# A feed-forward's down products computed by a second pass through DRAM, with seven instead of eight products

## The chip, the core and the metric

The kernel runs on one core of a Trainium2 chip. Its engines work side by side, each through its own queue of instructions in order: TensorE (PE) for matmuls, VectorE (DVE), ScalarE (ACT) and GpSimd (POOL) for everything element by element, SyncE (SP) mostly for issuing DMAs. The metric is the device time of one execution in microseconds (us), median of several.

## What is computed

One layer of an encoder, on 2048 tokens of one request and 256 of another (2304 in all, 1024 channels), in float32. Two mixers (a bidirectional mLSTM and an attention) come first and are not changed. The change lies in the last part of the layer and the final norm:

```python
x = x + jnp.concatenate([m_out, a_out], axis=-1) @ w_out
h = rmsnorm(x, norm2_w)
u = centred_dwconv(h @ w_up, conv_w, conv_b)      # 1024 -> 2 x 2816, width-3 convolution over tokens
a, g = jnp.split(u, 2, axis=-1)
x = x + (jax.nn.silu(g) * a) @ w_down             # 2816 -> 1024
return rmsnorm(x, final_norm_w)
```

The convolution is zero padded at the ends of each request.

## The kernel before

Channels lie on the 128 partitions and tokens along the free dimension. Every matmul is done three times: each operand is split into a rounded high part (a copy by ACT) and the rest (a difference, mostly by DVE), and high x high, high x low and low x high are summed in PSUM. The instructions are ordered at build by a scheduler that works with its own estimates of their durations; at run time every engine keeps that order.

Stage c (`phase_c`, L995) multiplies the mixed heads with `w_out`, nine blocks of 256 tokens, adds x, writes x to DRAM (`x1_d`, L1050) and the normed n2 to DRAM (`n2_d`, L1065). The operand tiles alternate between two rings (L1023).

The feed-forward (`phase_d`, L1221) runs over three blocks of 768 tokens (`BLK`). In each block the channels of the gate and of a go in 11 groups of two tiles (256 of 2816). The up product of two tiles and 1024 inputs is done as 2 x 2 blocks in seven products instead of eight (`up_start`, L1162): token halves and input halves give sums and differences. The sums of n2 are made once for a block by `n2_sums` (L1136): SP loads, POOL sums, SP stores to `n2t_d`, four calls, spread over groups 3 to 6 of the block before (L1348), or over stage c for the first block. `n2_load` (L1114) loads and splits the seven operands ("11", "21", "t2", "t1", "t3", "22", "t4"); three are loaded early, four at the start of the feed-forward, all seven anew at a block change. The sums of the weights are made by POOL for each pair of tiles (L1189 to L1192). Each of the seven weight tiles is split by ACT (L1180) and DVE (L1181) and used by 4 x 3 matmuls of 386, 384 or 382 columns (L1184). The products add up in three of four PSUM banks, and are copied out and added by ACT (L1200) and DVE (L1203) as the sums allow; "t2", "t3" and "t4" continue in the bank of "11".

The convolution (`conv`, L1265) is one ACT instruction (L1271) and two DVE instructions (L1278) a tile, with the tokens at a block's edge kept in `carry`. Then y (L1358) is silu(g) x a, split into `act` (L1363, L1364); `w_down` is loaded by SP (L1367) and split (L1373, L1374).

The down products (`down`, L1316) of a group are done one group later: 8 output tiles x 2 token parts, each 2 x 3 matmuls of 384 columns (L1322) in four banks of their own, added by DVE to accumulators in SBUF that hold x (L1324). So PE alternates between up and down products. After the last group of a block, `finish` (L1286) squares, sums, takes the power -0.5, spreads it over the partitions by matmuls (L142) and scales (L1312); SP stores y. In the last block the last two groups' down products go in three parts of 256 columns.

## Time and profile before

| | us |
|---|---|
| time, median of 3 runs | 3429.92 (3428.42 to 3431.00) |
| span of the profiled execution, first to last instruction | 3427.2 |
| feed-forward, from its first up matmul (1830.4) to the end | 1596.8 |
| one of the four groups from 2113.9 to 2299.7 | 46.5 |

The profiled execution's own time is known as its span; the median lies 2.7 us above it. A row such as "PE 3329.3 (97%) x20058" gives busy time, share of the span and number of instructions. PEld is the loading of weights into PE, which overlaps with matmuls. Matmuls overlap too, so their listed durations (some 338 ns for 384 columns) are longer than their distance in time; the distance is what counts, and is read from a number of them in a row. A "<-" behind an idle time names the instruction that ended it.

### The profile page before, as it was taken

To read this page: it belongs to the slowest core of one execution; us is meant where nothing else is said; L and a number is where in the kernel's file an instruction comes from. 1 tells how busy PE (TensorE), PEld (TensorE's weight loads), DVE (VectorE), ACT (ScalarE), POOL (GpSimd) and SP (SyncE) were. 2 spreads that over 40 slices of the span, in tenths; PEclk is the share of its full clock that TensorE was granted. 3 is DMA by queue.
4 is the path that set the end of the run, shared out by engine and by line. 5 is a ranking of instruction groups with operands and counts; after the bars stand their busy time and mean duration, and the time that the engine had idled before them with its cause. 6 is when DMAs were issued, how large, how long until landed. Compare 5 with 4: busy or idle time off the path is not lost. (4 is left out here: it accounts for less than half of the span.)

```text
span 3427.2 us, 55596 instructions
## 1 busy us (share of the span) xinstructions
PE 3329.3 (97%) x20058; PEld 3098.4 (90%) x20058; DVE 2677.3 (78%) x4654; ACT 1931.2 (56%) x4329; POOL 1120.9 (33%) x1328
## 2 busy tenths in 40 slices
PE   7989999999999999899999999999999999999998
PEld 6878888888888888688899999999999999999998
DVE  6885687777768788967767878789888888888776
ACT  4536666666666767655544444446444446555554
POOL 6653132213232323211244333226233224322222
PEclk9999999999999999999999999999999999999999
DMA  6765342333345444422365232223323213421221
GB/s 220 243 203 159 89 140 86 115 123 98 108 131 160 143 123 139 145 77 94 101 216 198 81 105 87 68 80 133 129 94 103 72 59 128 140 74 62 69 74 50
DMA packets 254756, 404.27 MB, mean 118 GB/s; under 512 B 32112, under 2 KB 156816, under 8 KB 254480
## 3 DMA queue, kind: packets, MB, share of 16 engines
q1 hardware_dynamic: 226576, 358.23, 32.7%
q0 software_dynamic: 11344, 33.04, 3.6%
q10 hardware_dynamic: 16560, 9.44, 0.9%
q8 instruction: 158, 2.59, 0.3%
q14 instruction: 118, 0.97, 0.1%
HBM read 316.73 MB, written 83.90 MB: 117 GB/s over the span
## 5 line engine op out<-in xcount | busy, mean ns | idle before, releaser
L1322 PE MATMUL pd<-act,wd 128*128 128x384 f32 (+1 forms) x3120 | 593.4, 336 | 23.9 <-DVE acc L1324 12.6
L1322 PEld LDWEIGHTS pd<-act,wd 128*128 128x128 f32 x3120 | 539.6, 188 | 32.6 <-DVE acc L1324 18.1
L601 DVE TENSOR_TENSOR pl<-ps,ph 128x512 fp32r<-128x512 f32 x520 | 352.7, 683 | 181.5 <-ACT ps L600 173.4
L1184 PE MATMUL pa<-nt,wut 128*128 128x386 f32 (+2 forms) x2376 | 454.3, 339 | 0.0
L599 ACT ACTIVATE ph<-ps 128x512 fp32r<-128x512 f32 x520 | 309.4, 595 | 243.5 <-PE ps L596 239.5
L1184 PEld LDWEIGHTS pa<-nt,wut 128*128 128x128 f32 x2376 | 421.6, 190 | 0.3 <-ACT u L1200 0.3
L570 DVE TENSOR_REDUCE mx<-px 128x1 f32<-128x512 f32 (+1 forms) x528 | 345.5, 670 | 74.4 <-PE px L569 72.4
L1278 DVE SCALAR_TENSOR_TENSOR y<-u,cw,y 128x768 f32<-128x768 f32 (+1 forms) x264 | 315.6, 1196 | 36.4 <-ACT y L1271 29.3
L1189 POOL TENSOR_TENSOR tw<-ru 128x512 f32<-128x512 f32 x66 | 94.1, 1425 | 732.5 <-DMA ru<-w_up 558.5
L613 PE MATMUL pv<-ph,v 128*128 128x512 f32 (+1 forms) x1040 | 319.4, 401 | 1.0 <-ACT ph L599 0.8
L600 ACT ACTIVATE ps<-ps 128x512 f32<-128x512 f32 x520 | 310.3, 597 | 0.0
L1200 ACT ACTIVATE u<-pa 128x386 f32<-128x386 f32 (+2 forms) x264 | 128.3, 486 | 320.9 <-PE pa L1184 320.7
L1324 DVE TENSOR_TENSOR acc<-pd,acc 128x384 f32<-128x384 f32 (+1 forms) x544 | 280.3, 535 | 35.5 <-PE pd L1322 34.1
L1041 PEld LDWEIGHTS po<-cmx,wo 128*128 128x128 f32 x1728 | 220.7, 191 | 8.2 <-DVE mmx L931 0.6
L1041 PE MATMUL po<-cmx,wo 128*128 128x256 f32 x1728 | 224.2, 284 | 0.4 <-DVE mmx L931 0.4
L595 PE MATMUL ps<-qq,kk 128*128 128x512 f32 x520 | 215.5, 416 | 4.2 <-DVE mx L570 2.4
L569 PE MATMUL px<-kk,qq 128*128 128x512 f32 (+1 forms) x528 | 202.8, 413 | 6.0 <-DVE mx L570 2.9
L596 PE MATMUL ps<-qm,kl 65*128 65x512 f32 x520 | 206.7, 399 | 0.0
L759 PE MATMUL mj<-mn,wm 128*128 128x256 f32 x1296 | 203.0, 289 | 2.8 <-ACT og L773 1.9
L759 PEld LDWEIGHTS mj<-mn,wm 128*128 128x128 f32 x1296 | 187.1, 193 | 19.8 <-ACT og L773 2.0
L769 PEld LDWEIGHTS mv<-wm,mn 128*128 128x128 f32 x1296 | 182.8, 190 | 18.4 <-ACT qb L765 2.5
L769 PE MATMUL mv<-wm,mn 128*128 128x256 f32 x1296 | 196.5, 285 | 1.0 <-ACT qb L765 0.9
(288 smaller groups left out, 7266.6 us busy)
## 6 DMA issues: line engine op xcount, KB each, us to landing
ru<-w_up SPq DMA_DIRECT2D x132, 512.0 KB, 3.4
mn<-n_d SPq DMA_DIRECT2D x216, 256.0 KB, 3.4
rd<-w_down SPq DMA_DIRECT2D x66, 512.0 KB, 3.6
n_d<-n1T SPq DMA_DIRECT2D x18, 1024.0 KB, 5.6
dm<-nm_d POOLq DMA_DIRECT2D x72, 256.0 KB, 4.1
mjn<-n_d SPq DMA_DIRECT2D x72, 256.0 KB, 3.3
mvn<-n_d SPq DMA_DIRECT2D x72, 256.0 KB, 3.1
q_d<-qz SPq DMA_DIRECT2D x18, 512.0 KB, 3.7
```

The lines of the kernel that those rows point to most:

```text
L570: nc.vector.tensor_reduce(s.mx[:, t, z0:z0 + 1], ps[:, 0:w], AX.X, ALU.max)
L599: nc.scalar.activation(ph, ps, AF.Exp)
L600: nc.scalar.activation(ps, ps, AF.Exp)
L601: nc.vector.tensor_tensor(pl, ps, f32(ph), ALU.subtract)
L613: nc.tensor.matmul(s.pv[0:HD if k in (1, 3) else P, 0:N], v, p, start=(kp == 0 and k == 0), stop=(2 * kp + 2 == s.nk and k == 5))
L759: nc.tensor.matmul(pj[:, o], s.w[c][:, a, o * P:(o + 1) * P], nT[c][:, :, h, :], start=(c + o + k == 0), stop=(c == NCC - 1 and k == 2 and ...
L769: nc.tensor.matmul(pv[:, o], nT[c][:, o, a, :], s.w[c][:, h, 256:512], start=(c + o + k == 0), stop=(c == NCC - 1 and k == 2 and o == 1))
L1041: nc.tensor.matmul(po[:, o], wo[z // 2][c][:, a, n], mx[c][:, h, :], start=(c == 0 and k == 0), stop=(c == NCC - 1 and k == 2))
L1184: nc.tensor.matmul(p, w[:, aa, c, :], ops[k][:, c, bb, 0:n], start=c == 0 and i == 0 and not add, stop=c == NCC // 2 - 1 and i == 2, skip_ ...
L1278: nc.vector.scalar_tensor_tensor(y[:, s:e], u[:, s + k:e + k], cw[:, k, jj:jj + 1], y[:, s:e], ALU.mult, ALU.add)
L1322: nc.tensor.matmul(po, wds[j][c // 4][:, aa, c % 4 * P:(c % 4 + 1) * P], acts[j][:, bb, z0:z1], start=(j == 0 and k == 0), stop=(j == len( ...
L1324: nc.vector.tensor_tensor(accs[c][:, z0:z1], po, accs[c][:, z0:z1], ALU.add)
```

## The change

The feed-forward becomes two passes. The up pass (`phase_u`) runs over two blocks of 1152 tokens. Each of the seven products is now 2 x 12 matmuls of 290 or 286 columns into a pair of banks, in a ring of four pairs that takes all eight banks; u22 is added by DVE directly from PSUM. From silu(g) x a of a group (two tiles, two token halves of 576) POOL makes the sums for seven down products and stores seven tiles of [128, 576] to DRAM (`a_d`). Nothing of the down product is done in this pass.

The down pass (`phase_e`) then runs over the seven products, in the order of `DOPS`. For each it goes over three stretches of 384 columns (1152 columns stand for both halves of both blocks) and 11 pairs of tiles, with 4 x 3 matmuls a pair, into two pairs of banks; the four result quadrants stay in SBUF and are updated after each stretch. Weights are loaded and split once, in a ring of 13; four of the seven weight tiles are sums, made by POOL in the first stretches and taken through DRAM (`s_d`). Operands come back from `a_d` by SP, four pairs at a time, split by ACT and DVE. POOL adds x and sums the squares; the norm follows in the steps after a stretch is complete.

Besides: `n2_sums` now issues its loads and stores from POOL, in halves, in a ring of three shared with the sums of the up pass; all splits of operands at the block change and the start go to DVE; x1 and n2 have other layouts (n2 in two tensors that overlap by 256 tokens); the two rings of stage c are swapped; rings and pools are placed in memory in a chosen order. The diff, cut to its core:

```diff
-BLK = 768
+BLK = 1152
...
-LAGO = 2
-AB = 3
-NH = 386
+NH = 580
 NW = 2 * NH + 1
-DT = (0, 2 * NH, 2 * NH + BLK, T)
+DT = (0, 2 * NH, T)
+HB = BLK // 2
+TW = T // 2
+N2A, N2B = 1280, 1024
+NP = NFC // 2
+CG = 384
 APRI = 1000
 WB = 8
 RST = 512
...
-WD = 4
 YB = 3
 UB = 3
 RW = 4
-PO = 4
-PB = 4
+WRA = 6
+WRB = 7
+TR = 4
+DW = 4
+TG = 4
+WA = 2
 PHB = 6
 PLB = 6
 PLAG = 2
-ZT = 3
 SG = 3
-RS = 2
 V, G = "vector", "gpsimd"
-P0 = ((V, G),) * 4
-P1 = ((V, G),) * 7
+P0 = ((V, V),) * 4
+P1 = ((V, V),) * 7
...
-                if n % 2:
+                if n % 2 == 0:
...
-            g.st.dma_start(g.x1_d[b, :, 2 * z - 2:2 * z + 2], x[:, 2 * z - 2:2 * z + 2])
+            g.st.dma_start(g.x1_d[:, 2 * z - 2:2 * z + 2, b * BT:(b + 1) * BT], x[:, 2 * z - 2:2 * z + 2])
...
-                g.st.dma_start(g.n2_d[:, z - 3:z + 1, b * BT:(b + 1) * BT], x[:, z - 3:z + 1])
+                if b * BT < N2A:
+                    g.st.dma_start(g.n2_d[0][:, z - 3:z + 1, b * BT:(b + 1) * BT], x[:, z - 3:z + 1])
+                if b * BT >= N2B:
+                    g.st.dma_start(g.n2_d[1][:, z - 3:z + 1, b * BT - N2B:(b + 1) * BT - N2B], x[:, z - 3:z + 1])
...
-            if n > 4 and sums:
+            if (n, z) > (5, 0) and sums:
...
-def n2_sums(g, pool, b, c, engs=("gpsimd",) * 4, tag="raw", bufs=RW):
+def n2_sums(g, pool, b, c, engs=("gpsimd",) * 4, tag="tc", bufs=3):
 
 
     nc = g.nc
     n = (DT[b + 1] - DT[b]) // 2
-    rs = []
-    for k in range(2):
-        r = pool.tile([P, D if tag == "raw" else 2 * NH], F32, tag=tag, name=f"rn{b}_{c}_{k}", bufs=bufs)[:, 0:2 * n]
-        r = r.rearrange("p (h t) -> p h t", h=2)
-        nc.sync.dma_start(r, g.n2_d[:, c + NCC // 2 * k, DT[b]:DT[b + 1]].rearrange("p (h t) -> p h t", h=2))
-        rs.append(r)
-    (b11, b12), (b21, b22) = ((r[:, 0], r[:, 1]) for r in rs)
-    for eng, (o, p, q) in zip(engs, ((b11, b12, b11), (b12, b22, b12), (b22, b22, b11), (b21, b21, b22))):
-        getattr(nc, eng).tensor_tensor(o, p, q, ALU.subtract)
-    for k in range(2):
-        g.st.dma_start(g.n2t_d[b, k, :, c, :, 0:n], rs[k])
-
-
-def up_load(g, s1, b, jj):
-
-    rs = [s1.tile([P, D], F32, tag="raw", name=f"ru{b}_{jj + k}", bufs=RW) for k in range(2)]
+    m = n // 2
+    for z in range(2):
+        rs = []
+        for k in range(2):
+            r = pool.tile([P, NH], F32, tag=tag, name=f"rn{b}_{c}_{z}_{k}", bufs=bufs)[:, 0:n]
+            r = r.rearrange("p (h t) -> p h t", h=2)
+            src = g.n2_d[b][:, c + NCC // 2 * k, DT[b] - (0, N2B)[b]:DT[b + 1] - (0, N2B)[b]].rearrange("p (h t) -> p h t", h=2)
+            nc.gpsimd.dma_start(r, src[:, :, z * m:z * m + m])
+            rs.append(r)
+        (b11, b12), (b21, b22) = ((r[:, 0], r[:, 1]) for r in rs)
+        for eng, (o, p, q) in zip(engs, ((b11, b12, b11), (b12, b22, b12), (b22, b22, b11), (b21, b21, b22))):
+            getattr(nc, eng).tensor_tensor(o, p, q, ALU.subtract)
+        for k in range(2):
+            nc.gpsimd.dma_start(g.n2t_d[b, k, :, c, :, z * m:z * m + m], rs[k])
+
+
+def up_load(g, pools, b, jj):
+
+    pool = pools[g.nup % 2]
+    g.nup += 1
+    rs = [pool.tile([P, D], F32, tag="raw", name=f"ru{b}_{jj + k}", bufs=2) for k in range(2)]
...
+def banks(g, pool, name):
+
+    k = g.nbank = g.nbank + 1
+    return pool.tile([P, 2, 512], F32, tag=f"p{k % 2}", name=name, bufs=1)
...
     def mul(p, k, src, add=False):
 
-        w = s1.tile([P, 2, NCC // 2, P], F32R, tag="wu", name=f"wu{k}_{nm}", bufs=WU)
+        i = g.nwu = (g.nwu + 1) % WU
+        w = s1[i // 3].tile([P, 2, NCC // 2, P], F32R, tag="wu", name=f"wu{k}_{nm}", bufs=3 if i < 3 else WU - 3)
         hi, lo = (w[:, a].rearrange("p c n -> p (c n)") for a in range(2))
         nc.scalar.activation(hi, src, AF.Copy)
         nc.vector.tensor_tensor(lo, src, f32(hi), ALU.subtract)
-        for c in range(NCC // 2):
-            for i, (aa, bb) in enumerate(((0, 0), (0, 1), (1, 0))):
-                nc.tensor.matmul(p, w[:, aa, c, :], ops[k][:, c, bb, 0:n], start=c == 0 and i == 0 and not add,
-                                 stop=c == NCC // 2 - 1 and i == 2, skip_group_check=add)
-    p1, p2 = bank("a"), bank("b")
+        for z in range(2):
+            for c in range(NCC // 2):
+                for i, (aa, bb) in enumerate(((0, 0), (0, 1), (1, 0))):
+                    nc.tensor.matmul(p[:, z], w[:, aa, c, :], ops[k][:, c, bb, z * m:z * m + m],
+                                     start=c == 0 and i == 0 and not add, stop=c == NCC // 2 - 1 and i == 2,
+                                     skip_group_check=add)
+    p1, p2 = bank("a" + nm)[:, :, 0:m], bank("b" + nm)[:, :, 0:m]
...
-        copy(u22, p1)
-        add(u22, u22, u21)
+        add(u22, p1, u21)
...
+            def store(k, gi, t):
+                nc.gpsimd.dma_start(g.a_d[gi // TG][DOPS.index(k), :, gi % TG, b * HB:(b + 1) * HB], t)
...
+                for y, yg in zip(yas, ygs):
+                    nc.vector.tensor_tensor(y, y, yg, ALU.mult)
+                b11, b12, b21, b22 = (y[:, k * HB:(k + 1) * HB] for y in yas for k in range(2))
+                t1, t2, t4 = (sa.tile([P, NH], F32, tag="tc", name=f"tc{k}_{b}_{gi}", bufs=3)[:, 0:HB] for k in (1, 2, 4))
+                store("11", gi, b11)
+                nc.gpsimd.tensor_tensor(t1, b12, b11, ALU.subtract)
+                nc.gpsimd.tensor_tensor(t2, b22, t1, ALU.subtract)
+                for k, t in (("t2", t2), ("21", b21), ("t1", t1)):
+                    store(k, gi, t)
+                nc.gpsimd.tensor_tensor(b12, b22, b12, ALU.subtract)
+                nc.gpsimd.tensor_tensor(t4, b21, t2, ALU.subtract)
+                for k, t in (("t3", b12), ("22", b22), ("t4", t4)):
+                    store(k, gi, t)
+
+
...
+def phase_e(g, tc, pd):
...
+    G3 = TW // CG
+    with ExitStack() as st:
...
+        quad = {k: sc.tile([P, 4, TW], F32, name="c%d%d" % k) for k in ((0, 1), (0, 0), (1, 0), (1, 1))}
...
+        def halves(t, src):
+            lo, hi = t[:, 1], t[:, 0]
+            nc.scalar.activation(hi, src, AF.Copy)
+            nc.vector.tensor_tensor(lo, src, f32(hi), ALU.subtract)
+
+        def down(f, o, p):
+            return g.w_down[0, (2 * p + f) * P:(2 * p + f + 1) * P, o * h:o * h + h]
+
+        SRC = {"11": (0, 0), "21": (1, 0), "t4": (1, 1)}
+        SUM = {"t1": 0, "t2": 1, "t3": 2, "22": 3}
+
+        def sums_load(p):
+            r = sy.tile([P, 4, h], F32, tag="x", name=f"ds{p}", bufs=2)
+            for k, (f, o) in enumerate(((0, 1), (1, 1), (0, 0), (1, 0))):
+                nc.gpsimd.dma_start(r[:, k], down(f, o, p))
+            return r
+
+        def sums(p, r):
+            b12, b22, b11, b21 = (r[:, k] for k in range(4))
+            nc.gpsimd.tensor_tensor(b22, b12, b22, ALU.add)
+            nc.gpsimd.tensor_tensor(b12, b11, b12, ALU.subtract)
+            nc.gpsimd.dma_start(g.s_d[SUM["t1"]][p], b22)
+            nc.gpsimd.tensor_tensor(b11, b22, b11, ALU.subtract)
+            nc.gpsimd.dma_start(g.s_d[SUM["t3"]][p], b12)
+            nc.gpsimd.tensor_tensor(b21, b21, b11, ALU.subtract)
+            nc.gpsimd.dma_start(g.s_d[SUM["t2"]][p], b11)
+            nc.gpsimd.dma_start(g.s_d[SUM["22"]][p], b21)
+
+        nw = [0]
+
+        def weight(i, p):
+            k = DOPS[i]
+            n = nw[0] % (WRA + WRB)
+            nw[0] += 1
+            w = (swa if n < WRA else swb).tile([P, 2, h], F32R, tag="w", name=f"we{k}_{p}", bufs=WRA if n < WRA else WRB)
+            r = sr.tile([P, h], F32, tag="dw", name=f"dw{k}_{p}", bufs=DW)
+            nc.sync.dma_start(r, down(*SRC[k], p) if k in SRC else g.s_d[SUM[k]][p])
+            halves(w, r)
+            return w
+
+        TS = [(p, min(p + TG, NP)) for p in range(0, NP, TG)]
+
+        def acts(i, z, q):
+            p0, p1 = TS[q]
+            t = sx.tile([P, 2, TG, CG], F32R, tag="t", name=f"te{DOPS[i]}_{z}_{q}", bufs=TR)[:, :, 0:p1 - p0]
+            nc.sync.dma_start(f32(t[:, 1]), g.a_d[q][i, :, :, z * CG:(z + 1) * CG])
+            halves(t, f32(t[:, 1]))
+            return t
...
+        def resid(o, hf, z):
+            x = sy.tile([P, 4, h], F32, tag="x", name=f"xe{o}{hf}_{z}", bufs=2)[:, :, 0:CG]
+            for c, n, t in spans(hf, z):
+                nc.sync.dma_start(x[:, :, c:c + n], g.x1_d[:, 4 * o:4 * o + 4, t:t + n])
+            a = C(o, hf)[:, :, z * CG:(z + 1) * CG]
+            nc.gpsimd.tensor_tensor(a, a, x, ALU.add)
+
+        done = set()
+
+        def squares(o, hf, z, ms=(0, 1, 2, 3)):
+            q = sy.tile([P, 4, h], F32, tag="x", name=f"qe{o}{hf}_{z}_{ms[0]}", bufs=2)[:, 0:len(ms), 0:CG]
+            nc.scalar.activation(q, C(o, hf)[:, ms[0]:ms[-1] + 1, z * CG:(z + 1) * CG], AF.Square, scale=1.0 / 32.0)
+            return [q[:, m] for m in range(len(ms))]
...
+        def norm(hf, z, extra=()):
+            ps = banks(g, pd[(g.nbank + 1) // 2 % 2], f"r{hf}_{z}")
+            sqs = [sms[hf, z], *extra]
...
+            for c in range(NCC):
+                a = C(c // 4, hf)[:, c % 4, z * CG:(z + 1) * CG]
+                nc.vector.scalar_tensor_tensor(a, a, g.fw[:, c:c + 1], r, ALU.mult, ALU.mult)
+                for c0, n, t in spans(hf, z):
+                    g.st.dma_start(g.yT[c, :, t:t + n], a[:, c0:c0 + n])
+
+        UPD = {"11": [((0, 1), None)], "21": [((0, 0), (0, 1))], "t4": [((1, 0), None)], "t2": [((0, 1), (0, 1))],
+               "t3": [((1, 1), (0, 1))], "t1": [((0, 1), (0, 1)), ((1, 1), (1, 1))], "22": [((0, 1), (0, 1))]}
...
+        fetch_w(WA)
+        fetch_t(2)
...
+        for p in range(NP):
+            if p + 1 < NP:
+                at(4 * p, lambda p=p: load_sums(p + 1))
+            at(4 * p + 1, lambda p=p: sums(p, sr4[p]))
+        for z in range(G3):
+            e = 2 * SZ + z * NP
+            at(e + 3, lambda z=z: resid(0, 0, z))
+            at(e + 8, lambda z=z: collect(0, z, squares(0, 0, z)))
+            e = 4 * SZ + (z + 1) * NP
+            at(e + 1, lambda z=z: resid(1, 0, z))
+            at(e + 3, lambda z=z: resid(0, 1, z))
+            at(e + 6, lambda z=z: collect(0, z, squares(1, 0, z)))
+            at(e + 14, lambda z=z: norm(0, z))
...
+        for i, k in enumerate(DOPS):
+            for z in range(G3):
+                end = i == 6 and z == G3 - 1
+                ps = [banks(g, pd[(g.nbank + 1) // 2 % 2], f"e{k}_{z}_{m}")[:, :, 0:CG] for m in range(2)]
+
+                def mul(p, ms):
+                    w, t = ws[i, p], ts[i, z, p // TG][:, :, p % TG]
+                    for m in ms:
+                        for n, (aa, bb) in enumerate(((0, 0), (0, 1), (1, 0))):
+                            nc.tensor.matmul(ps[m // 2][:, m % 2], w[:, aa, m * P:(m + 1) * P], t[:, bb],
+                                             start=p == 0 and n == 0, stop=p == NP - 1 and n == 2)
+
+                def update(m):
+                    def part(o, hf):
+                        return C(o, hf)[:, 2 * m:2 * m + 2, z * CG:(z + 1) * CG]
+                    for q, src in UPD[k]:
+                        if src is None:
+                            nc.scalar.activation(part(*q), ps[m], AF.Copy)
+                        else:
+                            nc.vector.tensor_tensor(part(*q), ps[m], part(*src), ALU.add)
+                    if k == "t3":
+                        nc.vector.tensor_tensor(part(1, 0), part(1, 0), part(1, 1), ALU.add)
+                n = (i * G3 + z) * NP
...
+                    norm(1, z, qs)
+                    continue
+                for p in range(NP):
+                    if p % TG == 0:
+                        fetch_t(1)
+                    mul(p, range(4))
+                    if i == 0 and z == 0 or z == G3 - 1:
+                        fetch_w(1)
+                    for f in todo.pop(n + p, ()):
+                        f()
+                for m in range(2):
+                    update(m)
+        assert not todo
...
-        dram("x1_d", [NB, P, NCC, BT])
+        dram("x1_d", [P, NCC, T])
+        g.a_d = [dp.tile([7, P, min(TG, NP - p), TW], F32, name=f"a_d{p}") for p in range(0, NP, TG)]
+        g.s_d = [[dp.tile([P, D // 2], F32, name=f"s_d{k}_{p}") for p in range(NP)] for k in range(4)]
...
-            phase_d(g, tc, s1, pd, ops, first)
+            pd.append(pool(s5, "d_v", bufs=1, space=PSUM))
+            phase_u(g, tc, s1, pd, ops, first)
+        phase_e(g, tc, pd)
```

259 lines of the change are left out of this document (137 added, 122 removed).

## The prediction

> **What bounds the kernel now.** I read the page first, for the engines' shares and the costliest groups.
>
> ```profile
> span 3427.2 us, 55596 instructions
> ...
> PE 3329.3 (97%) x20058; PEld 3098.4 (90%) x20058; DVE 2677.3 (78%) x4654; ACT 1931.2 (56%) x4329; POOL 1120.9 (33%) x1328
> ```
>
> PE is busy 97% of the span, so the question for every edit is what it does to PE's work and PE's gaps. Next comes the table by stretches, cut where the feed-forward changes its character. The columns are start and end, length, busy time with number of instructions for PE, PEld, DVE, ACT, POOL, then granted clock, DMA share and GB/s.
>
> ```profile
> 1700.00:1830.00 130.00, 128.77 (x948) 120.70 (x948) 79.03 (x131) 55.44 (x108) 50.76 (x45) 1.00 0.58 193
> ```
>
> ```profile
> 1830.40:1922.00 91.60, 88.96 (x502) 87.41 (x502) 79.42 (x104) 52.49 (x93) 40.03 (x24) 1.00 0.46 153
> 1922.00:2113.90 191.90, 187.72 (x1058) 185.32 (x1057) 154.86 (x206) 87.29 (x160) 70.21 (x48) 1.00 0.30 96
> 2113.90:2299.70 185.80, 185.80 (x1058) 185.80 (x1057) 150.86 (x212) 87.01 (x160) 49.57 (x32) 1.00 0.21 70
> 2299.70:2459.00 159.30, 151.64 (x850) 149.95 (x849) 137.34 (x183) 92.92 (x180) 72.72 (x48) 0.98 0.42 139
> 2459.00:2650.40 191.40, 186.14 (x1051) 183.09 (x1050) 157.64 (x208) 89.83 (x176) 68.44 (x48) 1.00 0.31 99
> 2650.40:2835.10 184.70, 184.70 (x1057) 184.70 (x1057) 149.26 (x209) 88.70 (x176) 49.42 (x32) 1.00 0.21 70
> 2835.10:2990.70 155.60, 145.44 (x818) 143.84 (x818) 137.89 (x180) 95.89 (x193) 71.89 (x47) 0.98 0.41 137
> 2990.70:3313.10 322.40, 322.40 (x1849) 322.40 (x1849) 256.72 (x364) 171.43 (x364) 83.09 (x56) 1.00 0.22 69
> 3313.10:3411.20 98.10, 98.06 (x665) 97.82 (x664) 75.60 (x134) 56.41 (x127) 21.41 (x22) 1.00 0.12 38
> 3411.20:3427.20 16.00, 4.66 (x20) 4.08 (x20) 6.05 (x18) 3.31 (x9) 3.58 (x5) 0.58 0.39 133
> ```
>
> The row from 2113.9 is four steady groups: PE busy 185.80 of 185.80 us. One group is two ups of 84 matmuls (386 columns) and 96 down matmuls (384), so 185.8 / (4 x 264) = 0.1759 us for a mean of 385.3 columns. A matmul of 256 columns is seen back to back at the end of the chain of waits: 19.83 / 168 = 0.1180 us.
>
> ```profile
> 3380.45 19.83 PE pd L1322 x168
> ```
>
> The line through both is 0.448 ns a column: 0.1754 us at 384 columns and 0.1323 us at 288. (Pure proportion would give 0.1315 at 288; the difference is the uncertainty.)
>
> Now the work before. The code has 3 blocks x 22 x 84 = 5544 up matmuls of 384 columns on average: 5544 x 0.1754 = 972.4 us. The down matmuls, grouped by shape:
>
> ```profile
> L1322 PE MATMUL pd<-act,wd 128*128 128x384 f32 x2976 | 575.5, 339 | 23.9 <-DVE acc L1324 12.6 <-DVE act L1364 6.3 <-ACT act L1363 3.5
> L1322 PE MATMUL pd<-act,wd 128*128 128x256 f32 x144 | 17.9, 281 | 0.0
> ...
> L1322 PE MATMUL pd<-act,n 128*128 128x256 f32 x72 | 12.4, 284 | 0.0
> L1322 PE MATMUL pd<-nt,n 128*128 128x256 f32 x72 | 12.3, 280 | 0.0
> ```
>
> 2976 x 0.1754 + 288 x 0.1180 = 556.0 us. So 1528.4 us of matmul work lies in the 1596.8 us from 1830.4 to the end; **68.4 us are unfilled**. By row, length less count x price (24 to 28 small norm matmuls taken off): start 4.7; the two stretches with operand sums 6.1 and 191.4 - 184.7 = 6.7; the two block changes 14.4 and 16.6; before the end 3; tail 16.0.
>
> **The change part by part.**
>
> *Matmuls.* Up: 2 blocks x 22 x 168 = 7392 of 288 columns: 978.0 us, 5.6 more than before (0 by pure proportion). Down: 7 products x 3 stretches x 11 pairs x 12 = 2772 of 384 columns: 486.2 us, 69.8 less. **PE work falls by 64.2 us**, to 1464.2. Norm matmuls: 18 column groups before, 18 after, nothing.
>
> *Seams.* One block change instead of two. Its operands are half as wide again (572 against 384 columns) and all conversions go to DVE: 15 us, within 10 to 25. Sums of block 1 in four groups instead of eight. Tail: the same chain of update, square, sum, power, rows, eight scalings and store: 15, within 12 to 17. Start: operands of 580 instead of 386 columns, all converted on DVE, while the first product needs one of them: 5, within 3 to 12. New is the seam from up to down: the last convolutions, products and stores stand before the last quarter of the first product, which PE reaches 8 x 12 x 0.1754 = 16.8 us later: 6, within 2 to 15.
>
> *DVE and POOL in the up pass.* A group has 336 x 0.1323 = 44.4 us of PE and no down matmuls beside it.
>
> ```profile
> L1181 DVE TENSOR_TENSOR wu<-ru,wu x132: 672/682/2030, 1782.7 to 3354.6; 128x512 fp32r<-128x512 f32 x132
> ```
> ```profile
> L1278 DVE SCALAR_TENSOR_TENSOR y<-u,cw,y x264: 997/1018/2303, 1853.0 to 3386.4; 128x768 f32<-128x768 f32 x88, 128x767 f32<-128x767 f32 x44
> ```
> ```profile
> L1358 DVE TENSOR_TENSOR y<-y,y x66: 941/958/1972, 1870.2 to 3388.7; 128x768 f32<-128x768 f32 x66
> ```
> ```profile
> L1191 POOL TENSOR_TENSOR ru<-ru,ru x66: 1287/1994/2023, 1787.1 to 3344.8; 128x512 f32<-128x512 f32 x66
> ```
> ```profile
> 2181.58 2.00 POOL L1192 TENSOR_TENSOR tw<-ru,tw 128x512 f32<-128x512 f32 x1
> ```
> ```profile
> 2182.36 1.77 DVE L1181 TENSOR_TENSOR wut<-tw,wut 128x512 fp32r<-128x512 f32 x1
> ```
> ```profile
> L1324 DVE TENSOR_TENSOR acc<-pd,acc x544: 409/545/559, 1888.7 to 3411.2; 128x384 f32<-128x384 f32 x166, 128x256 f32<-128x256 f32 x16
> ```
>
> The numbers are shortest, median and longest ns. DVE, scaled by length: 14 weight differences x 0.68, 8 convolution steps of 1152 x 1.53, 2 products x 1.44 = 24.6 us with both inputs in SBUF, and 6 additions from PSUM of 580 x 0.82 = 4.9. POOL: 8 weight sums x 1.29 and 4 new sums of 576 x 1.45 = 16.1. In the trace the two take turns: the difference at 2182.36 lasts 1.77 instead of 0.68 while POOL's instruction runs, whereas L1324, which reads PSUM, never passes 559 ns. Taking turns, 24.6 + 16.1 = 40.7 of 44.4 us: it fits, with little room. With the sums of block 1 (8 more of 286 columns, 0.72 each) it is 46.5, 2.1 over; four such groups give 8 us (6.4 if they lose what four lose today; up to 25 if POOL also stands waiting). ACT took 87.0 us in the four steady groups, 21.8 each. Even with every instruction half as long again (1152 for 768 columns) and none dropped it is 32.7 of 44.4 us: nothing.
>
> [...]
>
> *POOL's queue.* It gets the stores of the products (154), loads and stores of its sums (64, from SP) and of the weight sums (88), 306 in all.
>
> ```profile
> L856 POOL DMA_DIRECT2D dm<-nm_d x72: 536/607/659, 278.4 to 1406.8; - x72
> ...
> DMA to landing us min/median/max: 3.4/4.1/7.9
> ```
> ```profile
> POOL rn L1149 <- DMA rn<-n_d: 146.5, 15, 12.2
> ```
>
> At 0.607 us to issue, seven stores are 4.2 us a group: POOL then has 16.1 + 4.2 and its turns, some 24 to 28 of 44.4 us. POOL waits for its sums' loads today (146.5 us in 15 times, loads then queued on SP); now the load is issued by POOL itself, and the weight sums behind it, which PE's products t2, t1, 22 need, wait out the landing of about 4.1 us. They are due once in 22 us: hidden, unless several loads and stores of the three-buffer ring fall together; that is in the 25 above. SP loses these and gains 63 operand and 77 weight loads, at most 5 in a 23.2 us step at the ends of a product's weights: nothing. Bytes: seven stores of 128 x 576 x 4 B are 2.1 MB, beside 2.1 MB of up weights: 95 GB/s a group, where the row from 1830.4 moved 153. Nothing. In the down pass the weight sums take POOL 11 x (4 x 1.29 + 8 x 0.607) = 110 us of the first five steps (116); the first is loaded in the ninth: nothing.
>
> *Three y buffers.* The y of a group is now read by stores, so it comes free some 11 us of POOL work plus 4.1 us of landing after its product; the next is wanted about 22 us later. Hidden, barely: if it is late, ACT's first step of the convolution waits, with the copies from PSUM queued behind it.
>
> *PSUM.* Before, a stalled up product was covered by down matmuls. Now four pairs of banks serve a chain in which t2, t3 and t4 reuse one pair, with only one product (24 x 0.1323 = 3.2 us) between uses for a copy or an addition. The trace has one stretch of this kind, the first group, with nothing down to do yet (the gaps in brackets):
>
> ```profile
> 1859.99 2.38 PE L1184 MATMUL pc<-n,wu 128*128 128x386 f32 x12 [0.95 <-ACT u L1200]
> ...
> 1873.12 0.96 PE L1322 MATMUL pd<-act,wd 128*128 128x384 f32 x4 [0.50 <-ACT act L1363]
> ```
>
> 1.45 us in two ups, with only 12 x 0.176 = 2.1 us between uses. I take half per up, 0.36, for the longer product: 44 x 0.36 = 16 us, within 0 to 45.
>
> *Down pass.* A step is 132 x 0.1754 = 23.2 us. DVE at its fullest: 4224 columns of operand differences at 0.958 / 768, 5.3; 11 weights, 7.5; four updates of 768 columns, 4.4; a norm, 4.4: 21.6, and PE alternates between two halves of PSUM. 4 us in all, within 0 to 15. Scattered: 3. Earlier stages, where only rings and a queue change: nothing, as PE was busy 128.77 of 130 us; within 3 either way.
>
> **Sum.** Unfilled: 5 + 8 + 15 + 6 + 15 + 16 + 4 + 3 = 72, against 68.4. End: 1830.4 + 1464.2 + 72 = 3366.6, against the span 3427.2. The median shown is 3429.92, 2.7 above the span of the profiled execution, so I add 2.7: **3369.3 us**, 60.6 less.
>
> **The rivals.**
>
> *POOL and DVE pace the up pass.* For: 40.7 of 44.4 us, and all three engines in fixed order. Against: in the four steady groups DVE was busy 150.9 of 185.8 us, and PE never waited. If each up loses 1 us more, 44 us: 3413.
>
> *Slower: the bank chain breaks once in each up.* For: no cover, and a break costs more than itself:
>
> ```profile
> 2337.24 3.18 PE L1322 MATMUL pd<-act,wd 128*128 128x384 f32 x12 [2.46 <-DVE acc L1324]
> ```
> ```profile
> 2328.00:2337.00 9.00, 5.63 (x29) 4.98 (x29) 9.00 (x8) 4.31 (x8) 7.30 (x4) 1.00 0.48 146
> 2337.00:2341.00 4.00, 3.76 (x15) 3.76 (x16) 4.00 (x8) 0.32 (x1) 0.00 (x0) 0.68 0.13 20
> ```
>
> After 2.46 us of idling twelve matmuls take 3.18 instead of 2.12 us, at a granted clock of 0.68. Such a break in each up is 3.52 - 0.36 = 3.16 us, x 44 = 139: 3508. It decides from 60.6 / 44 + 0.36 = 1.7 us an up. Against: the first group lost 0.7 an up.
>
> [...]
>
> *The change doesn't bring what it says: the round trip starves the down pass.* Were each of 21 steps to begin with such a break, 21 x 3.52 - 4 = 70 us: 3439, no gain left. Against: operands are asked for two quarters ahead, 16.8 us, against some 4 us of landing.
>
> **How the numbers follow.** Forecast with 3345 to 3395 as its own range: 0.58. Below 3345 (the unknown terms near their low ends): 0.07. POOL and DVE: 0.17. Starved: 0.10. Bank chain: 0.08. A measurement of this kernel tells about 0.2%, 6.9 us, from no change. Faster by more: 0.58 + 0.07 + 0.15 of the second = 0.80; within: 0.02 of it and 0.06 of the starved = 0.08; slower: 0.04 + 0.08 = 0.12. The range, 3340 to 3426, leaves out the starved and the broken cases and the lowest ends.
>
> **What would show it.** Right: up groups of 44 to 45 us with PE full, down steps of 23 us, one seam of about 15 us. [...]

## The result, and the profile after

The changed kernel took 3391.2 us (median of 4 runs, 3389.41 to 3394.19) against 3429.17 for the kernel before beside it: a ratio of 0.989, 95% interval 0.9876 to 0.9904. The forecast was 3369.3 us; the time lies inside its range, the sign is right, and 22 us of the expected gain of 60.6 are missing. The profiled execution has a span of 3392.5 us, 25.9 above the sum of the forecast (3366.6). It is the slowest of the four runs (3394.19 us, 3.0 above their median), so some of the 25.9 is this execution's own.

The first two lines of the page of the changed kernel, engine by engine:

```profile
span 3392.5 us, 57175 instructions
...
PE 3276.5 (97%) x21402; PEld 3049.5 (90%) x21402; DVE 2426.0 (72%) x3759; ACT 1779.7 (52%) x3708; POOL 1360.6 (40%) x1684
```

PE's busy time fell by 52.8 us (3329.3 before) and its idle time rose from 97.9 to 116.0: most of the 64.2 us of work that the forecast took off is gone, and some of it came back as waiting. Where, the table by stretches of the changed kernel tells (columns as in the prediction: start and end, length, busy time with count for PE, PEld, DVE, ACT, POOL, then granted clock, DMA share, GB/s). The rows are the start of the up pass, two steady groups, two groups with operand sums, the block change, eight steady groups, and the seam to the down pass.

```profile
1851.10:1900.00 48.90, 40.58 (x264) 39.01 (x263) 35.59 (x37) 25.70 (x34) 17.72 (x11) 0.90 0.47 165
1900.00:1987.70 87.70, 87.70 (x653) 87.70 (x652) 65.78 (x59) 40.99 (x62) 44.47 (x38) 1.00 0.28 93
2075.40:2163.00 87.60, 85.16 (x633) 84.93 (x632) 77.58 (x57) 39.06 (x61) 66.25 (x68) 1.00 0.44 143
2339.00:2427.00 88.00, 84.58 (x632) 83.88 (x631) 80.56 (x68) 56.84 (x88) 43.95 (x33) 1.00 0.48 168
2500.00:2859.10 359.10, 359.10 (x2712) 358.90 (x2710) 253.93 (x239) 192.22 (x350) 158.65 (x147) 1.00 0.28 96
2859.10:2900.20 41.10, 30.11 (x155) 29.25 (x155) 32.83 (x25) 18.63 (x26) 24.98 (x30) 0.88 0.73 248
```

The row from 2500 is what the forecast called right: PE busy 359.10 of 359.10 us, 359.1 / 2712 = 0.1324 us a matmul, 44.5 us a group. The steady part of the change does what it was to do. The losses are at its edges, and the largest is not in the feed-forward at all: the first row begins at 1851.1, not at 1830.4.

The two longest waits of PE from 1300 to there (engine, line, what it waited for, us in total, times, longest):

```profile
PE po L1045 <- ACT cmx L1032: 11.2, 1, 11.2
PE rs_c L146 <- POOL rcol_c L139: 3.3, 1, 3.3
```

And the four longest in total of the feed-forward:

```profile
PE r L146 <- POOL rcol L1465: 9.1, 3, 7.5
PE pa L1202 <- ACT u L1220: 8.0, 6, 2.4
PE e L1531 <- ACT te L1373: 7.1, 1, 7.1
PE e L1531 <- DVE we L1374: 3.1, 1, 3.1
```

Four places, then: the first output product of stage c (11.2), the up pass's start, block change and single groups (8.0 in six waits), the first products of the down pass (7.1 and 3.1), and one normalisation in it (7.5).

### The profile page after: what moved, and what is told of

It reads as the page before. It is cut to its first block, busy times and chain, and to the rows that moved or that the text cites. A ratio compares the mean times of both kernels' runs of the same rounds, so it can differ in the third digit from the quotient of the medians.

```text
span 3392.5 us, 57175 instructions
## 1 busy us (share of the span) xinstructions
PE 3276.5 (97%) x21402; PEld 3049.5 (90%) x21402; DVE 2426.0 (72%) x3759; ACT 1779.7 (52%) x3708; POOL 1360.6 (40%) x1684
## 3 DMA queue, kind: packets, MB, share of 16 engines
q0 software_dynamic: 35824, 120.42, 10.8%
q8 instruction: 169, 2.77, 0.3%
## 5 line engine op out<-in xcount | busy, mean ns | idle before, releaser
L1202 PE MATMUL pa<-nt,wut 128*128 128x290 f32 (+1 forms) x3168 | 448.9, 298 | 10.1 <-ACT u L1220 8.0
L1202 PEld LDWEIGHTS pa<-nt,wut 128*128 128x128 f32 x3168 | 433.1, 190 | 12.1 <-ACT u L1220 9.4
L1312 DVE SCALAR_TENSOR_TENSOR y<-u,cw,y 128x1152 f32<-128x1152 f32 (+1 forms) x176 | 323.8, 1840 | 36.1 <-ACT yc L1310 17.3
L1531 PE MATMUL et<-tet,wet 128*128 128x384 f32 x1584 | 281.1, 338 | 1.3 <-DVE tet L1374 0.7
L1531 PEld LDWEIGHTS et<-tet,wet 128*128 128x128 f32 x1584 | 278.7, 189 | 1.9 <-DVE tet L1374 1.1
L1045 PE MATMUL po<-cmx,wo 128*128 128x256 f32 x1728 | 226.4, 285 | 11.4 <-ACT cmx L1032 11.2
L1531 PE MATMUL e<-te,we 128*128 128x384 f32 x1188 | 212.5, 339 | 11.0 <-ACT te L1373 7.1
L1531 PEld LDWEIGHTS e<-te,we 128*128 128x128 f32 x1188 | 210.0, 190 | 12.1 <-ACT te L1373 7.3
L617 PEld LDWEIGHTS pv<-ph,v 128*128 128x128 f32 (+1 forms) x1040 | 157.1, 163 | 37.3 <-ACT ph L603 1.8
```

The lines of the kernel that those rows point to most:

```text
L617: nc.tensor.matmul(s.pv[0:HD if k in (1, 3) else P, 0:N], v, p, start=(kp == 0 and k == 0), stop=(2 * kp + 2 == s.nk and k == 5))
L1045: nc.tensor.matmul(po[:, o], wo[z // 2][c][:, a, n], mx[c][:, h, :], start=(c == 0 and k == 0), stop=(c == NCC - 1 and k == 2))
L1202: nc.tensor.matmul(p[:, z], w[:, aa, c, :], ops[k][:, c, bb, z * m:z * m + m], start=c == 0 and i == 0 and not add, stop=c == NCC // 2 - 1 ...
L1312: nc.vector.scalar_tensor_tensor(y[:, s:e], u[:, s + k:e + k], cw[:, k, jj:jj + 1], y[:, s:e], ALU.mult, ALU.add)
L1531: nc.tensor.matmul(ps[m // 2][:, m % 2], w[:, aa, m * P:(m + 1) * P], t[:, bb], start=p == 0 and n == 0, stop=p == NP - 1 and n == 2)
```

## The 11 us ahead of the feed-forward: a turned condition

The wait of 11.2 us stands at the first product of the output projection. SP's timeline of the changed kernel (start, length, queue, line, transfer, count) shows its operands' loads:

```profile
1392.74 2.93 SPq L1031 DMA_DIRECT2D cmx<-mix_d  x4
...
1446.04 3.98 SPq L111 DMA_DIRECT2D ro<-w_out  x8
1450.18 5.64 SPq L1031 DMA_DIRECT2D cmx<-mix_d  x8
```

and PE's timeline the product that waited:

```profile
1456.50 0.58 PE L1045 MATMUL po<-cmx,wo 128*128 128x256 f32 x1 [11.22 <-ACT cmx L1032]
```

Eight operands `cmx` are loaded at 1392 and eight at 1450, so why wait? The order of the instructions in the built program has the answer, since it keeps the numbers of the token blocks, which the profile leaves out: in the changed kernel the eight early loads are block 1's, and block 0's come last, after the weights. The condition `n % 2 == 0` in `loads` sends block 0 to the ring `mx` instead of `nT`. Two theories were set against each other: R, this turned ring; and P, GpSimd, which in stage c now issues the loads of the n2 sums itself and is named in the second wait. Three kernels tell them apart.

**Ring put back (a)** in the changed kernel:

```diff
-                if n % 2 == 0:
+                if n % 2:
                     m = sp.tile([P, 2, BT], F32R, tag="mx", name=f"cmx{b}_{c}", bufs=MXB)
```

> Changed kernel with one condition put back: the first token block's operands of the output projection go to the normalised-input ring again, the second block's to the mixed-output ring. Theory R (ring): in the changed kernel SP issues block 0's eight operand loads only after the second half of w_out, at 1450.18, and TensorE waits 11.22 us for their split before its first output product at 1456.50; put back, that product starts at 1438 to 1442, the wait is under 1 us, and the last output product ends 11 to 16 us earlier, near 1836 to 1840 where it was 1851. Whether the end follows is a second question: if the ring was turned so that the up pass's operands find their memory free, the start of the up pass (14 us unfilled now) grows by 5 to 15 and the time is 3385 to 3395; if not, the time is 3374 to 3382. Rival P (GpSimd): the 19 us ahead of the feed-forward come from the n2 sums that GpSimd now loads itself in stage c; then the last output product still ends within 3 us of 1851 and the time stays at 3388 to 3394.

Measured: 3379.16 us, ratio 0.9863 (0.9842 to 0.9885), span 3380.6. PE's timeline of this kernel at the first output product:

```profile
1441.39 1.70 PE L1045 MATMUL po<-cmx,wo 128*128 128x256 f32 x12 [0.38 <-DVE mmx L935]
```

It starts 15.1 us earlier (11.1 against the changed kernel's second profile, below) and waits for something else, 0.38 us. The last output product starts at 1835.7 instead of 1851.0. R holds and P falls as the cause of the 11 us. By time alone the interval is clear of the changed kernel's second measurement (0.9913, below), not of its first (0.989); the wait that is gone decides. The second question is answered too: from the last output product to the first product of the down pass it is 1017.7 us here and 1015.2 in the changed kernel (1019.2 in its second profile, below). Putting the ring back costs the start of the up pass nothing that can be told from the scatter.

**The turned ring alone (b)**, in the kernel before (the same line, turned the other way):

> Kernel before with that one condition turned as in the change, nothing else. Theory R: first output product 11 to 16 us later than 1440.1, with a wait of about 11 us on the split of its first operand; time 3438 to 3444, less what an earlier free ring gives at the start of the feed-forward (0 to 6). Rival P: within 3 us of 3429, and no such wait.

Measured: 3436.6 us, ratio 1.003 (1.0021 to 1.004), so about 10 us slower. The wait is there, at the first output product, which starts at 1453.5:

```profile
PE po L1041 <- ACT cmx L1028: 11.5, 1, 11.5
```

The last output product starts at 1843.8 instead of 1830.3.

**Blocks 0 and 1 in one ring (c)**:

```diff
-                if n % 2 == 0:
+                if n % 2 == 0 and n:
```

> Changed kernel with blocks 0 and 1 both in the normalised-input ring and the last block still in the mixed-output ring. Theory R: no wait at the first output product (1438 to 1442); a wait of 3 to 7 us at block 1's first product, whose operands can load only when block 0's products have read their slots; the up pass starts as in the changed kernel; time 3379 to 3386. If the wait at block 1 is as long as the one taken away (11), 3388 to 3394. Rival P: 3388 to 3394 with the end of the output products where it is.

Measured: 3383.07 us, ratio 0.9863 (0.9836 to 0.989). The first output product starts at 1443.6, the last at 1837.7. The expected wait at block 1 did not come (0.9 us in all on splits of `cmx`, and one wait of 2.7 us on the addition at L1052): that block 1's operands load slot by slot while block 0's last products still run is the likely reason. So the early start and the early release of the other ring can both be had; run a shows no gain from the release.

**The changed kernel once more (k)**:

> The changed kernel itself once more, beside the kernel before. It tells how far one profiled execution stands from another: five kernels with the same program up to the feed-forward ended their last output product between 1845.7 and 1847.3, the changed kernel's first profile at 1851.0. If that one was late by chance, 1845 to 1848 here and a ratio of 0.988 to 0.991; if not, 1850 to 1852.

Measured: 3394.07 us, ratio 0.9913 (0.9896 to 0.9929), span 3390.9, last output product at 1845.6. The first profile's 1851.0 was late by chance, and that execution was late already ahead of stage c: SP's store to `mix_d` just before the first eight loads stands at 1390.41 in it, at 1386.26 in the second and at 1384.81 in the kernel before. (The ratio lies a little above the 0.988 to 0.991 that was expected with it.) Over the eight profiles of the changed kernel and its variants with the turned ring the mean is 1846.1 (1842.5 to 1851.0); with the ring put back it is 1835.7 and 1834.9 (the latter in the combined kernel, below). So the ring is worth 10.8 us of the 20.7 (13.5 in the kernel before, by run b); about 5 are that execution; the remaining 5 (1835.3 against 1830.3) come from something else ahead of the feed-forward. Who issues the loads and stores of the n2 sums is not it, by run f below (1845.7); the rest no run settled.

## The down pass: residual additions that stretch VectorE

The longest wait of the down pass is at its first normalisation. The timeline of the changed kernel there, GpSimd, VectorE and PE:

```profile
3205.99 4.15 POOL L1438 TENSOR_TENSOR c<-c,xe 128x1536 f32<-128x1536 f32 x1 [11.47 <-DVE c L1541]
3211.04 3.80 POOL L1438 TENSOR_TENSOR c<-c,xe 128x1536 f32<-128x1536 f32 x1 [0.90 <-DVE c L1543]
3217.81 1.26 POOL L1465 TENSOR_TENSOR rcol<-rcol,mhalf 128x3 f32<-128x3 f32 x1 [2.97 <-DVE rcol L1464]
...
3204.10 1.81 DVE L1541 TENSOR_TENSOR c<-et,c 128x768 f32<-128x768 f32 x2
3205.83 5.12 DVE L1543 TENSOR_TENSOR c<-c,c 128x768 f32<-128x768 f32 x2
...
3211.49 4.97 DVE L1374 TENSOR_TENSOR tet<-tet 128x1536 fp32r<-128x1536 f32 x1
...
3217.58 0.15 DVE L1464 TENSOR_SCALAR rcol<-r 128x3 f32<-128x3 f32 x1
...
3219.12 1.65 PE L146 MATMUL r<-ident,rcol 128*128 128x128 f32 x6 [7.54 <-POOL rcol L1465]
```

Read it from the bottom: PE waits for GpSimd's power (3217.81), that for VectorE's small step (3217.58), that stands behind a difference of 4.97 us, and that lies beside a GpSimd addition of 3.80. Two 768-column additions take 1.81 us at L1541, reading PSUM, and 5.12 at L1543, with both inputs in SBUF and GpSimd's 4.15 us addition beside them. Is it the order on GpSimd's queue (power behind additions), or the stretching?

**Order (d)**, the normalisation four steps earlier:

```diff
-            at(e + 14, lambda z=z: norm(0, z))
+            at(e + 10, lambda z=z: norm(0, z))
```

> Changed kernel with the normalisation of the first half of the token columns queued four steps earlier (10 steps after the end of t3's products where it was 14), ahead of the next residual additions. Theory N: TensorE waits 7.54 us at 3219 because the GpSimd power stands behind two residual additions of 4.15 and 3.80 us, and the DVE step before it behind a difference of 4.97 us that those additions stretch; put ahead of them the wait is under 1 us, the run of slow matmuls after it is gone, and the time is 3381 to 3385. Rival: the wait moves to the rows matmul at its new place or to the later normalisations, since the sums of squares arrive only then; then 3388 to 3394.

Measured: 3400.45 us, ratio 0.9923 (0.9903 to 0.9943), span 3395.3; the down pass takes 531.9 us from its first product to the end, where the changed kernel takes 526.3 (526.1 in its second profile). The time is above both ranges, though by its ratio not clear of the changed kernel's 0.9913. At its new place the first normalisation's wait is gone, as N has it, but a wait that neither named is there: PE now waits for VectorE's updates of the accumulators, which hold its banks.

```profile
PE et L1531 <- DVE c L1541: 7.5, 2, 4.9
```

**Stretching (e)**, the twelve residual additions on VectorE:

```diff
             a = C(o, hf)[:, :, z * CG:(z + 1) * CG]
-            nc.gpsimd.tensor_tensor(a, a, x, ALU.add)
+            nc.vector.tensor_tensor(a, a, x, ALU.add)
```

> Changed kernel with the six-by-two residual additions of the down pass (128x1536 each) on VectorE in place of GpSimd. Theory Q (the additions stretch VectorE): a GpSimd addition of about 4 us doubles and trebles what VectorE does beside it (768-column additions 2.56 us each where two others took 0.9, a 1536-column difference 4.97 where others take 1.76), and the power and the bank updates are late by that; on VectorE an addition takes 1.7 to 1.9 us, no VectorE step beside it is stretched, and the 7.54 us wait at the first normalisation falls under 2: 3383 to 3387. Rival O (order only): VectorE gains 12 steps of 1.8 us (21 us) in front of bank updates and operand splits, and TensorE waits there instead; the down pass stays at 526 us or grows: 3390 to 3400.

Measured: 3380.93 us, ratio 0.9868 (0.9854 to 0.9883), span 3380.5, some 2 us better than Q's range; the down pass takes 517.6 us, 8.7 less. The groups of VectorE around the first normalisation in this kernel (line, shapes, count, busy us, mean ns):

```profile
L1374 DVE TENSOR_TENSOR tet<-tet 128x1536 fp32r<-128x1536 f32 x5 | 8.8, 1755 | 17.7 <-ACT tet L1373 17.7
...
L1438 DVE TENSOR_TENSOR c<-c,xe 128x1536 f32<-128x1536 f32 x4 | 6.9, 1748 | 0.0
...
L1543 DVE TENSOR_TENSOR c<-c,c 128x768 f32<-128x768 f32 x4 | 3.6, 948 | 0.0
```

An addition costs VectorE 1.75 us; on GpSimd it cost some 4 us of GpSimd and 3.2 of VectorE's time besides (5.12 - 1.9, 4.97 - 1.76). All waits for the power in the feed-forward now sum to 2.6 us (9.1 in the changed kernel). Run e takes the additions off GpSimd's queue as well, so by itself it does not part the two theories; the rows above do. GpSimd stood idle for 2.97 us before the power, until VectorE's step, so its own queue did not hold the power back. Stretching was the cause, and engine work that looked free on an idle GpSimd was dearer than on the busier engine.

## The up pass: how much room the two engines' turns leave

The forecast's account of the up pass was that VectorE's and GpSimd's instructions with two inputs in SBUF take turns, 40.7 of 44.4 us a group (run j's expectation calls this the port account; the traces show the turns, not what causes them). PE was full, so the account says there are some 4 us left. Two kernels test it, and two more test choices that the change made beside it.

**GpSimd's weight sums twice (j)** (three of four in each up product; the result is the same):

```diff
-    nc.gpsimd.tensor_tensor(t1, a21, a22, ALU.add)
+    for _ in range(2):
+        nc.gpsimd.tensor_tensor(t1, a21, a22, ALU.add)
...
```

> Changed kernel with three of the four GpSimd weight sums of every up product done twice (same result): some 4.1 us more of two-input GpSimd work in each product, 8.2 in a group. By the forecast's port account (VectorE's and GpSimd's two-input work exclude each other, 40.7 us of a 44.4 us group taken) the group grows to 48 or 49 us and the time to 3460 to 3500. Rival: the account counts waiting as work, the two overlap in part, and TensorE stays full: 3388 to 3400.

Measured: 3479.55 us (one run, so no interval), span 3477.8. The eight steady groups' stretch of the changed kernel, in this one:

```profile
2500.00:2859.10 359.10, 338.85 (x2478) 336.86 (x2479) 289.40 (x224) 176.04 (x329) 248.01 (x184) 0.97 0.25 86
```

2478 matmuls in 359.1 us are 336 x 359.1 / 2478 = 48.7 us a group: the account's figure. GpSimd is busy 69% and VectorE 81% of the stretch, neither near full by itself, and these shares hold stretched instructions (a convolution step of 1152 columns takes 2.77 us on average). Counted instead with the shortest duration of each shape in the stretch (VectorE: 1.40 us a convolution step, 0.68 a weight difference, 1.35 a product; GpSimd: 1.28 a weight sum, 1.43 a sum of products), the two engines' work with both inputs in SBUF comes to some 350 of the 359.1 us here and to some 309 in the changed kernel: an estimate from these traces, and what taking turns would fill. Some 8 us more of GpSimd's work cost 4.2 a group, and the up pass takes 1106.5 us from the last output product to the first down product, against 1015.2.

**The fourth quarter of an up product copied first (i)**, as before the change:

```diff
-        add(u22, p1, u21)
+        copy(u22, p1)
+        add(u22, u22, u21)
```

> Changed kernel with the fourth quarter of an up product taken from PSUM as before: ScalarE copies the bank (0.65 us), VectorE adds from SBUF afterwards. The forecast charged 16 us for accumulation banks handed back late in the up products; the trace of the changed kernel shows a full TensorE there. Theory C (the direct addition set no bank free too late): steady stretch still 0.132 us a matmul without waits, the same time within 4 us: 3387 to 3395. Rival D: ScalarE's 44 extra copies (29 us in all) stand ahead of weight splits, and the waits for them in the groups with n2 sums and at the two operand loads grow: 3395 to 3405.

Measured: 3401.93 us, ratio 0.9933 (0.9919 to 0.9948), where the changed kernel beside it took 3394.07; the up pass, from the last output product to the first down product, takes 1027.4 us instead of 1015.2 and 1019.2. From 2500 to 2850 PE now loses 3.75 us where it lost nothing. The time lies in D's range, but the waits are not the ones that D named: PE waits for ScalarE's copies of the banks (16.5 us in 19 waits, 8.0 in 6 in the changed kernel), not for weight splits. In the steady groups these late copies stand right behind convolution steps for which ScalarE had itself waited 2.1 us on VectorE, and from 1900 to 2850 VectorE's busy time grew by 49.3 us, ScalarE's by 12.5. So VectorE's time is the likelier reason, which neither theory had; the run adds work to both engines and does not part them. Where VectorE's time goes, its groups of this kernel show:

```profile
L1223 DVE TENSOR_TENSOR u<-u 128x572 f32<-128x572 f32 x15 | 31.1, 2073 | 27.3 <-ACT u L1220 27.3
...
L1223 DVE TENSOR_TENSOR u<-pc,u 128x572 f32<-128x572 f32 x16 | 12.0, 749 | 11.3 <-PE pc L1202 11.3
```

The same addition of 572 columns takes 0.749 us with one input in PSUM and 2.073 on average with both in SBUF. Where GpSimd is idle (from 2582.07 to 2589.69) the latter is no slower; a row of the same kernel's timeline:

```profile
2588.20 0.76 DVE L1223 TENSOR_TENSOR u<-u 128x572 f32<-128x572 f32 x1 [1.96 <-ACT u L1220]
```

Reading the bank directly took this addition out of the turn-taking: in the changed kernel's eight steady groups none of the 49 additions from PSUM took more than 0.758 us, with GpSimd busy for 158.65 of the 359.1 us.

**Operand splits shared with GpSimd again (g)**:

```diff
-P0 = ((V, V),) * 4
-P1 = ((V, V),) * 7
+P0 = ((V, G),) * 4
+P1 = ((V, G),) * 7
```

> Changed kernel with every second difference of the up pass's operand splits on GpSimd again, at the start and at the block change. Theory V (VectorE alone is right): a GpSimd difference of 128x1160 takes 3 us or more, stretches VectorE's beside it, and each operand is ready later; the block change, 4 us unfilled in the changed kernel, costs 8 to 15, the start as much more: 3397 to 3408. Rival W: GpSimd is idle at both places, so the halves run side by side and TensorE starts earlier: 3384 to 3391.

Measured: 3405.58 us, ratio 0.9952 (0.9937 to 0.9968). Theory V holds. At the block change PE has one wait of 6.89 and one of 2.48 us, where the changed kernel has 1.22 and 0.55, and VectorE's own differences there, of the same shape, read

```profile
L1136 DVE TENSOR_TENSOR n<-n 128x1144 fp32r<-128x1144 f32 x3 | 13.6, 4527 | 2.1 <-ACT n L1135 2.1
...
L1136 DVE TENSOR_TENSOR nt<-nt 128x1144 fp32r<-128x1144 f32 x4 | 9.7, 2417 | 0.5 <-ACT nt L1135 0.5
```

against 1.56 and 1.47 us in the changed kernel. Half the differences given away, and the other half took longer than all of them had: 23.3 us here for 7, 21.0 there for 14.

**The loads and stores of the n2 sums on SP (f)**:

```diff
-            nc.gpsimd.dma_start(r, src[:, :, z * m:z * m + m])
+            nc.sync.dma_start(r, src[:, :, z * m:z * m + m])
...
-            nc.gpsimd.dma_start(g.n2t_d[b, k, :, c, :, z * m:z * m + m], rs[k])
+            g.st.dma_start(g.n2t_d[b, k, :, c, :, z * m:z * m + m], rs[k])
```

> Changed kernel with the loads and stores of the n2 sums (stage c and the groups 3 to 6 of the first block) on SP's queue again; sums stay on GpSimd. Theory L (own loads matter): on SP each load waits for its operand slot ahead of the weight loads of the next up product, so TensorE waits for weights in the four groups, 2 to 6 us each: 3398 to 3410. Rival M (they do not): SP's queue has slack, the four groups keep 44 to 45 us, and the waits for GpSimd's power at the end of stage c (3.3 and 1.7 us) go because its queue has fewer DMA issues ahead of it: 3386 to 3391.

Measured: 3387.73 us, ratio 0.989 (0.9876 to 0.9905). Rival M: the time is the same as with GpSimd's own loads, and PE has no wait in the groups that carry the sums (one of 2.44 us in the changed kernel). The up pass is shorter in this profile, 1011.3 us against 1015.2 and 1019.2, but the last output product is where it was (1845.7), and the times do not tell the two apart. Who issues these loads does not matter here.

## A version that is faster than both

**Combined (h):** ring put back, residual additions on VectorE, and the first weights and operands of the down pass split at a higher scheduling priority:

```diff
-        fetch_w(WA)
-        fetch_t(2)
+        with tc.high_priority(offset=1000):
+            fetch_w(WA)
+            fetch_t(2)
```

> Changed kernel with three edits: the ring condition put back, the residual additions on VectorE, and the first weights and operands of the down pass split at a higher scheduling priority (ahead of the last convolution of the up pass on ScalarE and VectorE). If the parts add: 12 less from the ring, 5 to 8 from the additions, 2 to 5 at the seam (its waits of 7.09, 0.78 and 3.12 us become 5 to 9 in all): 3366 to 3373. If the additions only move the wait: 3374 to 3380.

Measured: 3373.68 us, ratio 0.9849 (0.9833 to 0.9866), span 3368.8: between the two ranges. Stage by stage the parts add. The last output product is at 1834.9, 11.2 us ahead of the mean with the turned ring. The up pass takes 1018.5 us, as in the changed kernel's two profiles (1015.2 and 1019.2). The down pass takes 515.4 us, 10.9 less, where the additions alone gave 8.7 and the seam's three waits are 4.85, 1.00 and 2.42 us instead of 7.09, 0.78 and 3.12, 2.7 less. By ratios they would come to about 0.982 from the mean of 0.989 and 0.9913; 0.9849 is some 9 us above that, with intervals of 0.002 on each, so whether they overlap a little stays open in the times.

## Why the prediction was right, and where it was wrong

| Term of the sum | Forecast, us | Measured, us |
|---|---|---|
| start of the up pass | 1830.4, within 3 | 1851.1 (1845.7 in the second profile) |
| up matmuls | 978.0 | 985.7; 14 of them (1.9) ran ahead of 1851.1 |
| start | 5 | 14.5 |
| n2-sum groups | 8 | 2.4 in waits |
| block change | 15 | 3.4 in waits |
| PSUM chain | 16 | 0 in the steady groups |
| down matmuls | 486.2 | 0.1751 us each, as forecast |
| seam | 6 | 13.9 |
| down pass | 4 | 9.1 in waits for the power |
| tail | 15 | 14.9 |

The total came out within the range partly by luck, because the errors have both signs. By stretches, the 25.9 us are 20.7 ahead of the up pass and 22.2 from the last up product to the end (533.4 us, forecast 486.2 + 6 + 4 + 15), less 14.0 in the up pass (1008.0 us, forecast 978 + 5 + 8 + 15 + 16) and less the 3 that were put down as scattered. A price for PSUM banks that was not paid, and a block change that cost less, hid a good part of what the other two stretches lost.

*PE's work falls by 64.2 us.* Right in mechanism and nearly in size. The down matmul is 169.89 / 970 = 0.1751 us in a full stretch (0.1754):

```profile
3036.10:3206.00 169.90, 169.89 (x970) 169.89 (x971) 72.95 (x58) 56.72 (x59) 43.66 (x25) 1.00 0.53 169
```

The up matmul is 87.7 / 653 = 0.1343 at 290 columns and 0.1324 at 286, where the line gave 0.1323 on average: 3696 x (0.1343 + 0.1324) = 985.7, 7.7 more, so by these prices the work falls by 56.5 us. The line through 256 and 384 columns was a little low between them.

*"Earlier stages, where only rings and a queue change: nothing, as PE was busy 128.77 of 130 us; within 3 either way."* This step failed, by 20.7 us. The row quoted for it (1700 to 1830) is the end of stage c; the change acts at its beginning, 260 us earlier. A turned ring was read as a change of places, when it decides which block's operands are first in SP's queue. By runs a, b and k, 10.8 us of it are the ring and about 5 this execution; some 5 are open.

*Chain of PSUM banks, 16, and the slower rival.* The chain cost nothing in the steady groups: 2712 matmuls without a wait. This term failed: the half-per-up price was taken from two waits of the first group, which starts behind an operand load. The second of them (0.50, behind the split of `act`) is not of the chain at all, and the first (0.95, behind a copy) is the only wait of PE behind such a copy in the whole feed-forward of the kernel before. In the changed kernel waits behind such copies are 9.1 us in 7, nearly all at the start, in one group with sums and at the block change, which have terms of their own. The rival of a break in each up did not come.

*Start 5, block change 15.* Both off, in opposite directions. The start lost 48.9 - 256 x 0.1343 = 14.5 us (eight of the 264 are norm matmuls): six waits of 8.3 us in all, on ScalarE's copies, on splits and on the last block's normalisation, which stands among them, and slow matmuls after them (16 in 3.35 us at a granted clock of 0.62 behind the longest wait, of 2.07). The block change, with the same splits but nothing unfinished beside it, lost 3.4 in waits. That VectorE must do all differences is right by run g.

*Up pass paced by VectorE and GpSimd.* The forecast kept the account (40.7 of 44.4) and gave the overrun 0.17. The account holds: run j lands on it, and run i shows 1.3 us an up product of VectorE's time that the change had saved without the forecast pricing it. In the groups with sums, where it gave 46.5, only 2.7 us were lost in four groups; it was pessimistic there.

*Seam 6, within 2 to 15.* 41.1 - 155 x 0.1754 = 13.9. The forecast asked when the last quarter of a product is needed; the wait was at the first matmul, for splits on ScalarE and VectorE queued behind the last convolution. The priority in run h moved only 2 to 3 us of it.

*Down pass 4, starved rival 0.10.* After the seam no wait behind the splits of loaded operands is longer than 0.73 us, so the round trip through DRAM is hidden as forecast, and steps keep 23 us. What came instead was the 7.54 us at the normalisation. The list of VectorE's work in a step had differences, weights, updates and a norm, with no stretching; the account of turns was made for the up pass and not carried over. Run e shows that it should have been. The rest of the down pass's unfilled time (47.2 less 13.9, 9.1 and 14.9: 9.3) is mostly the norms' own 60 small matmuls, 6.7 us before the tail, for which the forecast's sum has no term; what is left is short waits and slow matmuls after waits (11 in 3.00 us from 3221.0, at a granted clock of 0.50, behind the wait of 7.54).

## What to carry to other kernels

A changed ring or queue is costed where it begins to act, not where a stage ends: ask which load is now issued last, and who is waiting for it. In this kernel two-input VectorE and GpSimd instructions with everything in SBUF acted as one budget (in run j some 8 us more of GpSimd's work cost 4.2 us a group with neither engine over 81% busy): add both engines' times in a stretch before moving work to an idle GpSimd, and look for operands that can be read from PSUM instead (0.749 us for an addition that took 2.073 on average with both inputs in SBUF, run i). A stall measured in one special place (here the first group) should not be multiplied by the number of places until the trace shows it in a second one.

## What the runs showed of the hardware

The granted clock after a wait did not follow the wait's length alone. Two waits of the changed kernel, each with the stretch of matmuls behind it:

```profile
1890.58:1892.60 2.02, 0.00 (x1) 0.00 (x0) 2.02 (x3) 1.71 (x3) 1.41 (x1) 1.00 0.00 0
1892.65:1896.00 3.35, 3.35 (x16) 3.35 (x17) 3.31 (x4) 1.12 (x2) 0.00 (x0) 0.62 0.02 5
...
2120.39:2122.80 2.41, 0.00 (x0) 0.00 (x0) 2.41 (x3) 1.73 (x3) 1.27 (x2) 1.00 0.41 122
2122.83:2126.30 3.47, 3.47 (x25) 3.47 (x26) 3.43 (x4) 1.71 (x3) 0.54 (x1) 1.00 0.00 0
```

After 2.02 us of idling the clock is 0.62 and 16 matmuls fit into 3.35 us; after 2.41 us it stays at 1.00 and 25 fit into 3.47. What decides was not tested.
